# A pair for adaLN units 18 and 19 inside the second value unit of a hybrid encoder layer

## The chip, the core and the metric

The kernel runs on one core of a Trainium2 chip. The time is the device time of one execution in microseconds, as the median of several runs. Times inside an execution come from the hardware profiler's trace; they count from the start of the span.

## What is computed

One encoder layer is computed for 1024 prompt frames and 32 sample frames (1056 columns in all), model width 1024, all in float32. What matters here:

```python
mod = jax.nn.silu(c) @ w_ada + b_ada
sh1, sc1, g1, sh2, sc2, g2 = jnp.split(mod[:, None, :], 6, axis=-1)
h = x * (1 + sc1) + sh1
mq, mk, mv, mo, mi, mf, fq, fk, fv, ff, gu, gv = jnp.split(h @ w_in, split_at, axis=-1)
...
mix = jnp.concatenate([hm, hf, hg], axis=-1) @ w_o
x = _layer_norm(ALPHA * x + (1 + g1) * mix, ln1_g, ln1_b)
h = x * (1 + sc2) + sh2
y = (jax.nn.silu(h @ w_gate) * (h @ w_up)) @ w_down
x = _layer_norm(ALPHA * x + (1 + g2) * y, ln2_g, ln2_b)
```

`mod` (the adaLN modulation) is a product of the two conditioning vectors with a matrix of 1024 x 6144. It is cut into 24 units of 256 columns: units 0 to 7 give sh1 and sc1, units 8 to 15 sh2 and sc2, units 16 to 19 g1, units 20 to 23 g2. g1 is needed only behind the mixers, at the output projection.

## The kernel before

**Engines and queues.** TensorE (PE) does all products, ScalarE (ACT) and VectorE (DVE) empty the PSUM banks and split operands, SyncE (SP) issues nearly all DMAs in one queue, in order. Each product is made of three (hi x hi, lo x hi, hi x lo), L402 to L404 in a value unit and L130 to L132 elsewhere. The program text gives the data flow; a scheduler sets the order of each engine from it, within some fixed dependencies, and so one edit can move instructions that its lines don't name. Each DMA of SP also waits, on its lane (DMAHW0 to DMAHW7), for the DMA issued eight before it.

**An adaLN unit.** `ada_load` (L186) loads the 256 columns as two tiles of 512 KB (L87). `ada_parts` (L193) multiplies them (L202, 8 matmuls in the program, 16 records in the trace), copies the sum from its bank (ACT, L206), transposes it twice on PE (L211), reduces it on DVE (L213), and adds the bias (L219, L223). Up to four units can share one bank, one copy and the two transposes; a group of two is called a pair here.

**The value units.** After the first stage (units 0 to 7 with the first part of the input projection, to about 59 us) come two value units, calls of `tm_unit` (L389) with 264 columns each: the values of the attention heads and the gate columns. A unit has a sample tile (L416) and then tiles 0 to 7, each of 24 products into one of three banks of the pool `pg`. `evac_v` (L423) empties a tile: ACT copies the bank to `tm_traw` (L434, two buffers); SP stores that to the output (`o_v`, 128 KB, L91); DVE splits it into `tm_vhl` (L440, L441, two buffers); SP stores this to `start_dv` (256 KB). So a copy can run only when the store of the tile two before it has landed.

**Where the later adaLN units stand.** Units 16 and 17 are a pair of the function `group` in `run`: its loads go into the pool `pe` (tag `early`, EB = 4 buffers, one unit takes two), and `tie` fixes the matmuls on PE behind tile 0 of the second value unit. `rest` lists the units that follow as single units through `more`: 18 and 19 behind the first step of the gates (`T1[3]` = 2), and 8 to 15 at the eight `a` of ORDER. Their loads go into the pool `pl` (tag `late`, two buffers), so one unit's loads wait until the unit before is done. Behind the value units come the gate columns, the attention heads (`head`, `fox`), the mLSTM chunks, the output projection and the feed-forward part, which takes most of the span.

Of the kernel before, what the change touches and what calls it, by code (L numbers as in the profile page):

```python
# [32 lines left out]
LWE = 1  # L33
NB = (3, 2, 2)
PRE = 5
EB = 4
T1 = (0, 0, 0, 2)
XB, AB = (3, 6)
HPA = 200
MLB = (1, 2, 3, 4, 5)  # L40
# [29 lines left out]
class Kernel:  # L70
# [1428 lines left out]
    def run(self):  # L1499
# [53 lines left out]
        sl = ExitStack()  # L1553
        self.pl = self.pada = self.pool("pl", ctx=sl)
        w1 = d["w_in_v"]
        rest = [18, 19] + list(range(8, 16))

        def more(n):
            for u in rest[:n]:
                self.ada((u,), self.pl, "late", 2, self.pt, "t")  # L1560
            del rest[:n]

        more(T1[0])
        se = ExitStack()
        pe = self.pool("pe", ctx=se, side="right")

        def group(units):
            def go():
                first = len(nc.cur_bb.bb.instructions)
                target = self.lastmm  # L1570
                for _ in self.ada_parts(units, raws, self.pt, "t"):
                    pass
                self.tie(nc.cur_bb.bb.instructions[first:], target, (mybir.EngineType.PE,))
                self.phase = "tm"
            raws = [self.ada_load(u, pe, "early", EB) for u in units]
            return go

        self.tm_unit(w1[0], 264, self.evac_v(0))
        self.tm_unit(w1[1], 264, self.evac_v(1), between={0: group((16, 17))})
        se.close()  # L1580
        s2 = ExitStack()
        self.mx = self.pool("mx0", ctx=s2)
        more(T1[2])
        gates = self.gates()
        next(gates)
        more(T1[3])
        self.foxbufs = (2, 2, 2, 2, 3)
# [278 lines left out]
```

## Time and profile before

| what | value |
|---|---|
| median of 3 runs | 1346.33 us (1344.91 to 1347.18) |
| profiled execution, its own time | 1346.69 us |
| its span from first to last instruction | 1344.9 us |
| PE, ACT, DVE busy | 98%, 49%, 74% of the span |
| granted TensorE clock, mean | 0.998 |
| first value unit's last product on PE | 82.69 us |
| matmuls of units 16 and 17 | 88.01 us |
| matmuls of unit 18 and of unit 19 | 131.45 us and 140.99 us |

A row of the windows view gives a stretch, and the busy time of each engine in it with the number of instructions. A row of a timeline gives start, duration, engine, line, operation, output and inputs, and in brackets how long the engine idled before it and what ended that. `SPq` is the queue on which SP issues DMAs; a row there is the issue, not the transfer. Busy time of matmuls is modelled, so that the steps from start to start say more than durations.

### The profile page before, as it was taken

Reading aid. Unit: us, or ns where it says so; the run is one execution under the profiler, and the core shown is the slowest. Engines: PE = TensorE matmul, PEld = TensorE weight load, DVE = VectorE, ACT = ScalarE, POOL = GpSimd, SP = SyncE. Lnnn points to the kernel's source line nnn. Section 1 sums busy time; section 2 is a strip of 40 time slices with the busy share of each in tenths; the row PEclk is TensorE's granted clock in tenths of the full one; section 3 lists DMA queues with packets and bytes.
Section 4 is the critical chain, followed back from the end, with each engine's and each line's share of the span. In section 5 each row is a group of like instructions: output and inputs, shape, how many; then the busy total and the mean of one; then the engine's idle time right before and its main releaser. Section 6 shows DMA issues by size and latency. Waiting matters only on the chain.

```text
span 1344.9 us, 25607 instructions
## 1 busy us (share of the span) xinstructions
PE 1324.0 (98%) x9684; PEld 1208.3 (90%) x9684; DVE 989.1 (74%) x2091; ACT 655.8 (49%) x1305; POOL 231.9 (17%) x263
## 2 busy tenths in 40 slices
PE   9999999999999999999999999999999999999996
PEld 6798888888999888888888888999999999999995
DVE  5635655678779667686876776678979887988777
ACT  3413445455547545545454454435754453635355
POOL 0102100143246100000000001464610000000341
PEclk9999999999999999999999999999999999999999
DMA  9585465546557754454344332663785858554221
GB/s 362 207 299 154 150 204 186 174 131 207 181 195 257 191 136 130 117 163 126 115 121 116 110 104 82 217 175 112 205 231 154 228 148 225 139 175 131 89 79 67
DMA packets 119450, 221.73 MB, mean 165 GB/s; under 512 B 18580, under 2 KB 62768, under 8 KB 119328
## 3 DMA queue, kind: packets, MB, share of 16 engines
q1 hardware_dynamic: 112096, 207.55, 49.0%
q0 software_dynamic: 6032, 11.94, 5.2%
q8 instruction: 76, 1.25, 0.4%
q10 hardware_dynamic: 1200, 0.62, 0.2%
q14 instruction: 46, 0.38, 0.1%
HBM read 188.13 MB, written 51.85 MB: 178 GB/s over the span
## 4 chain that ended last, share of the span: by engine, by line
PE 68%; DVE 4%; DMA 1%; ACT 1%; issue 1%; DVEq 0%; ACTq 0%
PE up_g L130 6%; PE up_g L132 6%; PE up_g L131 6%; PE dn_g L130 4%; PE dn_g L132 4%; PE dn_g L131 4%; PE sup_u L132 3%; PE sup_u L131 3%; PE sup_u L130 3%; PE wo_g L131 2%; PE wo_g L132 2%; PE wo_g L130 2%; PE sup_g L132 2%; PE sup_g L131 2%; PE sup_g L130 2%; PE fox_t L943 2%
## 5 line engine op out<-in xcount | busy, mean ns | idle before, releaser
L130 PE MATMUL up_g<-tm_ah,up_whi 128*128 128x512 f32 (+1 forms) x384 | 140.0, 365 | 0.0
L131 PE MATMUL up_g<-tm_al,up_whi 128*128 128x512 f32 (+1 forms) x384 | 140.0, 365 | 0.0
L132 PE MATMUL up_g<-tm_ah,up_wlo 128*128 128x512 f32 (+1 forms) x384 | 139.7, 364 | 0.0
L1368 ACT CAST sup_whi<-sup_raw 128x1024 fp32r<-128x1024 f32 x54 | 56.1, 1048 | 89.3 <-PE dn_u L131 43.9
L130 PEld LDWEIGHTS up_g<-tm_ah,up_whi 128*128 128x128 f32 x384 | 72.3, 188 | 11.1 <-DVE tm_al L1246 0.4
L132 PEld LDWEIGHTS up_g<-tm_ah,up_wlo 128*128 128x128 f32 x384 | 72.3, 188 | 11.1
L131 PEld LDWEIGHTS up_g<-tm_al,up_whi 128*128 128x128 f32 x384 | 72.3, 188 | 10.7
L916 ACT ACTIVATE fox_p<-fox_s,fox_fmx 128x384 f32<-128x384 f32 (+2 forms) x96 | 55.2, 579 | 53.0 <-DVE fox_fmx L914 41.2
L1199 DVE SCALAR_TENSOR_TENSOR wo_z<-dn_g,start_mod,wo_z 128x512 f32<-128x512 f32 (+4 forms) x120 | 60.3, 521 | 22.6 <-PE dn_g L132 22.0
L118 DVE TENSOR_TENSOR up_wlo<-up_raw,up_whi 128x1024 fp32r<-128x1024 f32 x50 | 65.2, 1305 | 15.0 <-ACT up_whi L117 13.7
L1369 DVE TENSOR_TENSOR sup_wlo<-sup_raw,sup_whi 128x1024 fp32r<-128x1024 f32 x54 | 68.0, 1263 | 10.7 <-ACT sup_whi L1368 10.7
L117 ACT CAST up_whi<-up_raw 128x1024 fp32r<-128x1024 f32 x50 | 52.4, 1048 | 47.2 <-PE up_g L131 23.9
L130 PE MATMUL dn_g<-up_acth,dn_whi 128*128 128x512 f32 (+2 forms) x200 | 73.5, 368 | 0.8 <-DVE wo_z L1199 0.8
L132 PE MATMUL dn_g<-up_acth,dn_wlo 128*128 128x512 f32 (+2 forms) x200 | 73.3, 366 | 0.0
L131 PE MATMUL dn_g<-up_actl,dn_whi 128*128 128x512 f32 (+2 forms) x200 | 72.8, 365 | 0.0
L948 ACT CAST fox_pth<-fox_t 128x512 fp32r<-128x512 f32 (+1 forms) x80 | 41.6, 542 | 59.2 <-PE fox_t L943 57.5
L117 ACT CAST dn_whi<-dn_raw 128x1024 fp32r<-128x1024 f32 (+1 forms) x44 | 42.7, 971 | 51.7 <-PE up_g L131 16.0
L911 DVE TENSOR_REDUCE fox_fmx<-fox_s 128x1 f32<-128x384 f32 (+2 forms) x96 | 52.8, 553 | 16.3 <-PE fox_s L908 15.0
L949 DVE TENSOR_TENSOR fox_ptl<-fox_t,fox_pth 128x512 fp32r<-128x512 f32 (+1 forms) x80 | 49.9, 631 | 15.9 <-ACT fox_pth L948 15.6
L118 DVE TENSOR_TENSOR dn_wlo<-dn_raw,dn_whi 128x1024 fp32r<-128x1024 f32 (+1 forms) x44 | 49.5, 1125 | 10.4 <-ACT dn_whi L117 9.5
L402 PE MATMUL tm_g<-tm_whi,start_h1h 128*128 128x256 f32 (+1 forms) x192 | 55.3, 288 | 0.7 <-DVE tm_traw L477 0.7
L1320 POOL DMA_DIRECT2D start_dp<-w_gu x19 | 19.8, 1067 | 209.0 <-DMA start_dp<-w_gu 209.0
(684 smaller groups left out, 4799.7 us busy)
## 6 DMA issues: line engine op xcount, KB each, us to landing
up_raw<-w_gu SPq DMA_DIRECT2D x50, 512.0 KB
ada_late<-w_ada SPq DMA_DIRECT2D x28, 512.0 KB
dn_raw<-w_dn SPq DMA_DIRECT2D x28, 512.0 KB
sup_raw<-w_gu SPq DMA_DIRECT2D x20, 512.0 KB
start_dp<-w_gu SPq DMA_DIRECT2D x19, 512.0 KB
start_dp<-w_gu POOLq DMA_DIRECT2D x19, 512.0 KB, 8.0
wo_raw<-w_o SPq DMA_DIRECT2D x18, 512.0 KB
sup_raw<-start_dp SPq DMA_DIRECT2D x18, 512.0 KB
```

The costliest lines, as they stand in the source:

```text
L117: nc.scalar.copy(hi[:, :w], raw[:, :w])
L118: (eng or nc.vector).tensor_tensor(lo[:, :w], raw[:, :w], f(hi[:, :w]), ALU.subtract)
L130: nc.tensor.matmul(ps, hi, xh(k), start=start and k == 0, stop=False)
L131: nc.tensor.matmul(ps, hi, xl(k), start=False, stop=False)
L132: self.lastmm = nc.tensor.matmul(ps, lo, xh(k), start=False, stop=stop and k == n - 1)
L402: nc.tensor.matmul(ps[:, :ncol], xh, hi, start=k == 0, stop=False)
L911: nc.vector.tensor_reduce(mxs[:, x:x + 1], s[:, :w], AX.X, ALU.max, negate=True)
L916: nc.scalar.activation(pr[:, lo:hi], banks[x][:, :hi - lo], AF.Exp, bias=mxs[:, 0:1], accum_out=sums[:, x:x + 1])
L949: nc.vector.tensor_tensor(pl[:, :e], ps[:, :e], f(ph[:, :e]), ALU.subtract)
L1199: self.lastz = self.nc.vector.scalar_tensor_tensor(z[:, m, x:y], ps[:, x - a:y - a], g[i], z[:, m, x:y], ALU.mult, ALU.add)
L1368: nc.scalar.copy(h, x)
L1369: tt(l, x, f(h), ALU.subtract)
```

## The change

Units 18 and 19 leave `rest` and become a second pair of `group`. Its loads are asked for when tile 0 of the second value unit has been written down, behind the first pair; its matmuls are tied behind tile 5 (the sixth). `EB` goes from 4 to 8, so that both pairs have buffers of their own. `T1[3]` goes to 0, and units 8 to 15 keep their places at the `a`.

```diff
-EB = 4
-T1 = (0, 0, 0, 2)
+EB = 8
+T1 = (0, 0, 0, 0)
...
-        rest = [18, 19] + list(range(8, 16))
+        rest = list(range(8, 16))
...
         self.tm_unit(w1[0], 264, self.evac_v(0))
-        self.tm_unit(w1[1], 264, self.evac_v(1), between={0: group((16, 17))})
+        pairs = [group((16, 17))]
+        self.tm_unit(w1[1], 264, self.evac_v(1), between={
+            0: lambda: (pairs[0](), pairs.append(group((18, 19)))), 5: lambda: pairs[1]()})
         se.close()
```

The order of each engine shows what moves. On SP, in the first value unit: the stores of tiles 3 and 4 of the output are `o_v<-tm_traw_854` and `o_v<-tm_traw_887`, the split values' stores are `start_dv`, and `w_ada` is read by the adaLN loads (`tm_early` for the pairs, `ada_late` for single units: unit 18 before, unit 8 after).

```order
 L91 DMA start_dv_59<-tm_vhl_825 128x512
-L87 DMA ada_late_1420<-w_ada 128x1024
-L87 DMA ada_late_1422<-w_ada 128x1024
+L87 DMA tm_early_1117<-w_ada 128x1024
+L87 DMA tm_early_1119<-w_ada 128x1024
 L91 DMA o_v<-tm_traw_854 128x256
+L87 DMA tm_early_1121<-w_ada 128x1024
 L91 DMA start_dv_59<-tm_vhl_858 128x512
+L87 DMA tm_early_1123<-w_ada 128x1024
+L87 DMA ada_late_1819<-w_ada 128x1024
+L87 DMA ada_late_1821<-w_ada 128x1024
 L91 DMA o_v<-tm_traw_887 128x256
```

Unit 18's two loads are replaced by the pair's first two, and four loads of 512 KB come between the stores of tiles 3 and 4. A little ahead of these rows, the first early load of units 16 and 17 now waits for lane DMAHW0 beside its own, which is the lane of the store of `fm_x` from the stage before; before, the store of tile 2 was the first to wait for it.

On ACT, at the end of the first value unit: 920, 953 and 986 are the copies of tiles 5, 6 and 7, `tm_tmsum` that of the second unit's sample tile, 1080 that of its tile 0.

```order
 L434 COPY tm_traw_920<-tm_g_895 128x264 [waits DVE_49,DMAHW6_49,PE_49,Activation_49]
 L117 CAST tm_whi_1010<-tm_raw_1008 128x1056 [waits PE_49]
-L434 COPY tm_traw_953<-tm_g_928 128x264 [waits DMAHW0_49,DVE_49,Activation_49]
-L117 CAST ada_whi_1466<-ada_raw_1464 128x1024 [waits PE_49]
-L434 COPY tm_traw_986<-tm_g_961 128x264 [waits DMAHW2_49,DVE_49,Activation_49]
+L117 CAST gates_whi_1459<-gates_raw_1457 128x1024 [waits PE_49]
 L420 COPY tm_tmsum_1047<-tm_g_1014 32x66 [waits PE_49]
 L420 COPY tm_tmsum_1047<-tm_g_1014 32x66 x3
-L434 COPY tm_traw_1080<-tm_g_1055 128x264 [waits DVE_49,DMAHW4_49,PE_49,Activation_49]
+L434 COPY tm_traw_953<-tm_g_928 128x264 [waits DMAHW4_49,DVE_49,Activation_49]
+L434 COPY tm_traw_986<-tm_g_961 128x264 [waits DMAHW6_49,DVE_49,Activation_49]
```

The copies of tiles 6 and 7 now stand behind those of the sample tile; the lane that the copy of tile 6 waits for is still that of tile 4's store, under another number.

On PE, the new place of units 18 and 19, after the last product of tile 5 (`tm_g_1257`) and ahead of tile 6 of the second value unit:

```order
L404 MATMUL tm_g_1257<-tm_whi_1010,start_h1l_172 128x264
L202 MATMUL ada_t_1290<-tm_early_1119,start_c_62_182 32x256 x4
L202 MATMUL ada_t_1290<-tm_early_1123,start_c_62_182 32x256 x4
L202 MATMUL ada_t_1290<-tm_early_1121,start_c_62_182 32x256 x4
L202 MATMUL ada_t_1290<-tm_early_1117,start_c_62_182 32x256 x4
L402 MATMUL tm_g_1319<-tm_whi_1004,start_h1h_171 128x264
```

And the old place of unit 18 on PE, inside a product of a head's second unit (unit 19 stood the same way some 9 us later, and each had its two transposes):

```order
L130 MATMUL fm_g_1757<-start_h1h_171,gates_whi_1709 128x272
L202 MATMUL ada_t_1424<-ada_late_1422,start_c_62_182 32x256 x4
L202 MATMUL ada_t_1424<-ada_late_1420,start_c_62_182 32x256 x4
L131 MATMUL fm_g_1757<-start_h1l_172,gates_whi_1709 128x272
```

The 16 matmuls now stand together, with one pair of transposes behind them in place of two. From there (104.8 us in the trace of before) to 262 us the pieces of attention, the gates and units 8 and later stand at other places between the same products; ahead of and behind that stretch PE's order is the same in both programs.

## The prediction

> **What bounds the kernel now.** The page comes first: its first part, and the shares of the chain that ended last.
>
> ```profile
> span 1344.9 us, 25607 instructions
> PE 1324.0 (98%) x9684; PEld 1208.3 (90%) x9684; DVE 989.1 (74%) x2091; ACT 655.8 (49%) x1305; POOL 231.9 (17%) x263
> PE 68%; DVE 4%; DMA 1%; ACT 1%; issue 1%; DVEq 0%; ACTq 0%
> ```
>
> TensorE (PE) is busy for 98% of the span, so any time PE stands still is time added at the end, unless a later stall shrinks by as much. The second view is the table of windows, over the stretches in which the order of PE differs (up to 262 us) and the one behind.
>
> ```profile
> 68.00:77.00 9.00, 9.00 (x76) 9.00 (x76) 1.78 (x7) 1.14 (x3) 0.00 (x0) 1.00 1.00 310
> 77.00:82.00 5.00, 5.00 (x43) 5.00 (x43) 0.76 (x3) 0.00 (x0) 0.00 (x0) 1.00 1.03 409
> 82.00:84.00 2.00, 1.34 (x32) 1.12 (x35) 0.38 (x2) 0.80 (x2) 0.00 (x0) 1.00 0.56 206
> 84.00:86.00 2.00, 1.87 (x64) 1.71 (x54) 1.87 (x5) 2.00 (x5) 0.00 (x0) 1.00 0.52 193
> 86.00:105.00 19.00, 19.00 (x174) 17.92 (x173) 7.63 (x34) 3.05 (x11) 0.00 (x0) 1.00 0.77 258
> 105.00:262.00 157.00, 155.90 (x1261) 136.99 (x1261) 93.83 (x265) 77.79 (x183) 13.42 (x22) 1.00 0.55 169
> 262.00:450.00 188.00, 185.30 (x1610) 175.22 (x1609) 150.85 (x347) 99.40 (x216) 82.21 (x84) 1.00 0.62 198
> ```
>
> The columns are window, length, busy us of PE, PEld, DVE, ACT and POOL, granted clock, DMA share, GB/s. From 68 to 82 us the DMA engines are full (share 1.00 and 1.03) while PE is full as well; right behind, at 82 to 86 us, PE loses 0.66 + 0.13 us. The third view, the timelines of SP's queue, ACT and PE, says why.
>
> ```profile
> 68.35 1.29 SPq L87 DMA_DIRECT2D tm_early<-w_ada  x2
> 70.93 0.34 SPq L91 DMA_DIRECT2D o_v<-tm_traw  x1
> 71.32 1.19 SPq L87 DMA_DIRECT2D tm_early<-w_ada  x2
> 72.62 0.51 SPq L91 DMA_DIRECT2D start_dv<-tm_vhl  x1
> 73.19 1.23 SPq L87 DMA_DIRECT2D ada_late<-w_ada  x2
> 74.76 0.37 SPq L91 DMA_DIRECT2D o_v<-tm_traw  x1
> 76.06 0.33 SPq L91 DMA_DIRECT2D start_dv<-tm_vhl  x1
> 76.87 0.34 SPq L91 DMA_DIRECT2D o_v<-tm_traw  x1
> ```
>
> ```profile
> 76.46 0.38 ACT L434 COPY tm_traw<-tm_g 128x264 f32<-128x264 f32 x1 [4.68 <-DMA o_v<-tm_traw]
> 83.20 0.38 ACT L434 COPY tm_traw<-tm_g 128x264 f32<-128x264 f32 x1 [6.37 <-DMA o_v<-tm_traw]
> 83.48 1.08 ACT L117 CAST tm_whi<-tm_raw 128x1056 fp32r<-128x1056 f32 x1
> 84.46 0.38 ACT L434 COPY tm_traw<-tm_g 128x264 f32<-128x264 f32 x1
> ```
>
> ```profile
> 82.69 0.29 PE L404 MATMUL tm_g<-tm_whi,start_h1l 128*128 128x264 f32 x1
> 83.64 1.13 PE L416 MATMUL tm_g<-tm_raw,start_hs 128*32 128x66 f32 x64 [0.66 <-ACT tm_traw L434]
> 84.89 0.39 PE L402 MATMUL tm_g<-tm_whi,start_ah 128*128 128x264 f32 x1
> ```
>
> I count the tiles of a value unit from 0. The copies at 76.46, 83.20 and 84.46 empty the banks of tiles 4, 5 and 6 of the first value unit. The one at 83.20 had waited 6.37 us for the store of tile 3, because traw has two buffers. That store was issued at 74.76 and holds 131 KB, which is 0.3 us at 409 GB/s; it took 8.4 us since it stood behind six loads of 512 KB. PE's sample tile at 83.64 needs the bank that this copy frees, since the products have three banks in turn; tile 0 of the second unit, at 84.89, needs the bank of tile 6, copied at 84.46, which in turn needs the store of tile 4 (issued 76.87). So here the program is at the edge already: **PE waits for ACT, ACT for a small store, the store for big loads.**
>
> **The change part by part.** *Removed PE work.* Two single units become a pair.
>
> ```profile
> 131.23 0.29 PE L130 MATMUL fm_g<-start_h1h,gates_whi 128*128 128x272 f32 x1
> 131.45 1.07 PE L202 MATMUL ada_t<-ada_late,start_c 128*32 128x256 f32 x16
> 132.68 0.28 PE L132 MATMUL fm_g<-start_h1h,gates_wlo 128*128 128x272 f32 x1
> 132.81 0.29 PE L130 MATMUL fm_g<-start_h1h,gates_whi 128*128 128x272 f32 x1
> ...
> 87.80 0.28 PE L404 MATMUL tm_g<-tm_whi,start_al 128*128 128x264 f32 x1
> 88.01 1.93 PE L202 MATMUL ada_t<-tm_early,start_c 128*32 128x256 f32 x32
> 90.11 0.29 PE L403 MATMUL tm_g<-tm_wlo,start_ah 128*128 128x264 f32 x1
> ...
> 135.33 0.29 PE L132 MATMUL fm_g<-start_h1h,gates_wlo 128*128 128x272 f32 x1
> 135.46 0.38 PE L211 MATMUL ada_t<-start_ident,ada_adas 128*128 128x128 f32 x2
> 135.80 0.28 PE L131 MATMUL fm_g<-start_h1l,gates_whi 128*128 128x272 f32 x1
> ```
>
> A single unit costs PE 132.68 - 131.23 = 1.45 us less two ordinary steps of 0.125, so 1.20. A pair costs 90.11 - 87.80 = 2.31 less two steps of 0.12, so 2.07. Two transposes cost 135.80 - 135.33 = 0.47 less two steps, so 0.22. The saving is 2 x 1.20 - 2.07 + 0.22 = **0.55 us**. One copy on ACT and one reduction with its share of small operations on DVE go too; ACT (49%) and DVE (74%) have room there, so I cost them at nothing.
>
> *Moved loads.* This is the term that decides. In the new order of SP four loads of 512 KB (the second unit of the pair, and unit 8, whose buffers are now free from the start) stand between the stores of tiles 3 and 4 of the first unit; before, none did. They are 4 x 524,288 B = 2.10 MB. At 409 GB/s, the rate of the same stretch, they take 5.13 us; at the 310 GB/s of 68 to 77 us, 6.77 us. I take 409, since they would run right behind that stretch, in a queue as full. Issue is no limit: the DMA that the tile 4 store's lane waits for is the first load of the pair, five big transfers earlier.
>
> Before, the store of tile 4 landed after 83.20 and before 84.46; behind the store of tile 3 it had one store of 262 KB and its own 131 KB to move, 0.96 us at 409 GB/s, so I take 84.16 (an estimate from these rows). After, it lands at 84.16 + 5.13 = 89.29. From the start of a copy to PE is 83.64 - 83.20 = 0.44 us, so tile 0 starts at 89.73 and not at 84.89: **+4.84 us**. The ends are +3.9 (landing just after 83.20) and +6.5 (310 GB/s). Behind the waiting copy on ACT stand the copy of tile 7 and then the pair's own copy; on PE stands everything.
>
> *The later start of the train.* With the new pool the first early load also waits for the store of fm_x (lane DMAHW0). Before, that lane's next user, the store at 70.93, had it by then, and the load had gone at 68.35. So the start slips by 0 to 2.6 us. The queue was full but slow then (310 against 409 GB/s), so most of a slip is caught up: I take +0.4 us.
>
> *No second stall.* The copy of tile 7 waits for tile 5's store, which follows tile 4's after 0.4 MB (about 1 us); the bank that it frees is needed 2.9 + 2.07 us after 89.73. The first copy of the second unit waits for tile 6's store, which stands behind three weight loads (1.57 MB, 3.9 us) and lands near 96; its bank is needed by tile 3, near 100. The loads of units 18 and 19 land near 88 and are used near 109. So I cost these at nothing; without the margin every 512 KB ahead of a store would cost 1.28 us.
>
> *The order from 105 to 262 us* is reshuffled: attention and adaLN pieces stand at other places between the same products. Before, PE idles there for 157.00 - 155.90 = 1.10 us, so at most that can go; the stretch behind it idles 2.70 of 188.00, and a new order could cost 1.6 more. Bounds -1.1 to +1.6; I take 0. Behind 262 us the order of PE is the same to the end, and it passes a shift on: 86 to 105 is full, and the idle of 105 to 450 (3.8 us) waits on engines that PE feeds.
>
> **Sum:** -0.55 + 4.84 + 0.4 + 0 = +4.69 us on the profiled execution's 1346.69 (span 1344.9 and 1.8 around it), 1351.4 us. The median of the runs shown is 0.36 lower than that execution, so I forecast 1351.0.
>
> [...]
>
> **The rivals.** *The stall also slows the clock (0.22).* From the end of the sample tile to 89.73 PE would stand still for about 4.9 us, a length that the trace shows only once.
>
> ```profile
> 1332.00:1334.00 2.00, 1.21 (x6) 0.67 (x4) 0.68 (x2) 0.82 (x3) 0.00 (x0) 1.00 0.01 4
> 1336.00:1338.00 2.00, 0.00 (x0) 0.00 (x0) 1.93 (x6) 1.31 (x3) 0.00 (x0) 1.00 0.00 0
> 1338.00:1341.00 3.00, 0.00 (x0) 0.00 (x0) 2.90 (x8) 2.35 (x5) 0.00 (x0) 0.54 0.56 186
> ```
>
> At the end PE's last matmul ends near 1333.2; the granted clock stays at 1.00 past 1338 and has a mean of 0.54 to 1341, so it fell to half near 1338.2, after 5.0 us. My gap is just under that. If it falls, the next tile (24 products, from 84.89 to a step behind 87.80, 3.0 us) runs at half speed and costs 3.0 more: 1354.0 us. [...]
>
> *The stores do not wait for the loads (0.12).* If packets of the small store get through between the loads, tile 4's store lands by 84.46 as before and only the saving is left: 1345.8 us, not slower. It decides at one point: does the store land within 0.4 us of the old time? For it speaks only that no view lists the packets one by one, so the order inside the queue is inferred. Against it: the store at 74.76 took 8.4 us behind six loads, and the one at 70.93, for which the copy at 76.46 waited, 5.5 us behind two.
>
> *The stall is partly given back (0.16).* The landing at its early end (-0.9) and the idle time of 105 to 262 us gone (-1.1): 1349.0 us, on the border of 0.2%. That the pair might not form is no rival: the order of PE shows its 32 matmuls behind tile 5.
>
> **How the numbers follow.** The forecast has 0.50, and the time is its 1351.0. Less than 0.2% (2.7 us) is about what a measurement of this kernel can tell from no change. The forecast and the clock rival are slower (0.72), and half of the give-back (0.08), less 0.02 for luck in the reshuffled order: 0.78. Same: most of the free-store case and the other half, 0.19. Faster needs 2.7 us, with no stall, where the saving and the bound of the reshuffled order give 1.65: 0.03, for bounds that are wrong. The range 1347.3 to 1354.5 takes in give-back, clock rival and the bounds that do not all fall together; it leaves out the free-store case and the far upper end.
>
> **What would show it.** Right: in ACT's timeline a wait of tm_traw for the o_v store that ends near 89, and PE's tile 0 of the second unit starting near 89.7 with 4 to 6 us idle before it, the rest shifted by a constant. The SP queue then shows o_v behind four loads, and the pair of units 18 and 19 one insertion of 2.07 us near 109. Wrong: a tile 0 start before 86; a granted clock under 1.00 in 88 to 95 (the clock rival); or idle time in 105 to 262 that moves by more than 1.6 us.

## The result, and the profile after

The changed kernel takes 1349.55 us in the median of 13 runs (1345.07 to 1351.83), the kernel before 1346.12 us (13 runs, 1344.05 to 1348.96). The ratio is 1.0024, with a 95% interval of 1.0015 to 1.0032: slower by 3.2 us (2.0 to 4.3). The sign held, and the time lies in the range, 1.5 us under the forecast of 1351.0 us. The sum behind it did not hold term by term: two of its terms were wrong by about the same amount in opposite directions.

The page of the changed kernel shows nothing of this; PE is at 98% as before.

```profile
span 1347.8 us, 25594 instructions
PE 1324.7 (98%) x9682; PEld 1210.0 (90%) x9682; DVE 988.9 (73%) x2090; ACT 656.0 (49%) x1304; POOL 233.5 (17%) x263
```

The windows around the stall do (columns as in the prediction: window, length, PE, PEld, DVE, ACT, POOL, granted clock, DMA share, GB/s):

```profile
82.00:84.00 2.00, 1.18 (x10) 0.96 (x8) 0.15 (x1) 0.00 (x0) 0.00 (x0) 1.00 1.04 405
84.00:86.00 2.00, 1.13 (x64) 0.96 (x64) 0.45 (x2) 1.66 (x3) 0.00 (x0) 1.00 1.03 418
86.00:88.00 2.00, 0.56 (x2) 0.56 (x3) 2.00 (x3) 1.35 (x5) 0.00 (x0) 0.57 1.02 410
88.00:90.00 2.00, 2.00 (x11) 2.00 (x10) 0.92 (x4) 0.00 (x0) 0.00 (x0) 0.50 1.08 412
90.00:92.00 2.00, 2.00 (x11) 2.00 (x10) 0.91 (x4) 0.76 (x2) 0.00 (x0) 0.50 0.99 358
92.00:94.00 2.00, 2.00 (x25) 1.39 (x28) 0.11 (x1) 0.00 (x0) 0.00 (x0) 0.72 0.99 330
94.00:96.00 2.00, 2.00 (x29) 1.40 (x22) 0.00 (x0) 0.37 (x1) 0.00 (x0) 1.00 0.83 309
```

Two things are to be seen. PE loses 0.82 + 0.87 + 1.44 us in the first three windows, where the kernel before lost 0.79 in all. And the granted clock is at half from 86 to 93 us: in 88 to 90 us PE is "busy" all the time with 11 matmuls, where the kernel before has 17 to 19 in each 2 us from 90 to 96 us at a clock of 1.00. The DMA queue is full from 82 to 90 us (share 1.02 to 1.08, 405 to 418 GB/s); that it stands behind both is what the experiments test.

ACT's timeline, at the end of the first value unit:

```profile
84.34 0.38 ACT L434 COPY tm_traw<-tm_g 128x264 f32<-128x264 f32 x1 [7.43 <-DMA o_v<-tm_traw]
84.61 1.08 ACT L117 CAST tm_whi<-tm_raw 128x1056 fp32r<-128x1056 f32 x1
85.59 1.05 ACT L117 CAST gates_whi<-gates_raw 128x1024 fp32r<-128x1024 f32 x1
86.53 0.85 ACT L420 COPY tm_tmsum<-tm_g 32x66 f32<-32x66 f32 x4
90.58 0.38 ACT L434 COPY tm_traw<-tm_g 128x264 f32<-128x264 f32 x1 [3.19 <-DMA o_v<-tm_traw]
```

The first and the last row are the copies of tiles 5 and 6. They started at 83.20 and 84.46 before; now the second waits for the store of tile 4 until 90.58. That is the long wait for an `o_v` store that the prediction asked for. But PE did not wait for that copy:

```profile
82.89 0.29 PE L404 MATMUL tm_g<-tm_whi,start_h1l 128*128 128x264 f32 x1
84.77 1.13 PE L416 MATMUL tm_g<-tm_raw,start_hs 128*32 128x66 f32 x64 [1.59 <-ACT tm_traw L434]
87.44 0.59 PE L402 MATMUL tm_g<-tm_whi,start_ah 128*128 128x264 f32 x1 [1.54 <-ACT tm_tmsum L420]
92.67 0.42 PE L404 MATMUL tm_g<-tm_whi,start_al 128*128 128x264 f32 x1
93.02 1.95 PE L202 MATMUL ada_t<-tm_early,start_c 128*32 128x256 f32 x32
95.13 0.29 PE L403 MATMUL tm_g<-tm_wlo,start_ah 128*128 128x264 f32 x1
```

Tile 0 of the second unit starts at 87.44, released by the copies of the sample tile (L420), which end there; tile 6's copy comes 3.1 us later. Tile 0 then runs from 87.44 to 92.89, with 0.22 us between steps in place of 0.12 (11 matmuls in 88 to 90 us).

To follow the shift, the same instruction is read in both traces. The last product of the first unit stands at 82.69 before and 82.89 now (0.20 apart since the first stage of the run). The L403 behind the first pair stands at 90.11 before and 95.13 now, 5.02 later. So the stall and the slow tile cost 4.82 us together: 2.55 - 0.20 = 2.35 to the start of tile 0 (84.89 to 87.44), and 2.47 from there to the pair and tile 1. Of the 2.35 us, 0.93 came ahead of the sample tile (1.59 us idle in place of 0.66). The rest came behind it: its matmuls ended at 85.90, and its copies started only at 86.53, behind the two casts on ACT.

### The profile page after: what moved, and what is told of

It reads as the page before. It is cut to its first block, busy times and chain, and to the rows that moved or that the text cites. A ratio compares the mean times of both kernels' runs of the same rounds, so it can differ in the third digit from the quotient of the medians.

```text
span 1347.8 us, 25594 instructions
## 1 busy us (share of the span) xinstructions
PE 1324.7 (98%) x9682; PEld 1210.0 (90%) x9682; DVE 988.9 (73%) x2090; ACT 656.0 (49%) x1304; POOL 233.5 (17%) x263
## 4 chain that ended last, share of the span: by engine, by line
PE 69%; DVE 4%; DMA 2%; issue 0%; ACT 0%; SPq 0%; DVEq 0%; ACTq 0%
PE up_g L130 6%; PE up_g L132 6%; PE up_g L131 6%; PE dn_g L130 4%; PE dn_g L132 4%; PE dn_g L131 4%; PE sup_u L132 3%; PE sup_u L131 3%; PE sup_u L130 3%; PE wo_g L130 2%; PE wo_g L132 2%; PE wo_g L131 2%; PE sup_g L131 2%; PE sup_g L132 2%; PE sup_g L130 2%; PE fox_t L943 2%
## 5 line engine op out<-in xcount | busy, mean ns | idle before, releaser
L402 PE MATMUL tm_g<-tm_whi,start_ah 128*128 128x256 f32 (+1 forms) x192 | 56.3, 294 | 2.1 <-ACT tm_tmsum L420 1.5
L404 PE MATMUL tm_g<-tm_whi,start_al 128*128 128x256 f32 (+1 forms) x192 | 55.6, 290 | 0.0
```

Source lines behind the costliest of these rows:

```text
L402: nc.tensor.matmul(ps[:, :ncol], xh, hi, start=k == 0, stop=False)
L404: self.lastmm = nc.tensor.matmul(ps[:, :ncol], xl, hi, start=False, stop=k == 7)
```

## Where the shift goes later

Further on two rows of PE are compared: the first sample tile behind 320 us, and the last matmul of the run. The kernel before:

```profile
322.72 1.10 PE L416 MATMUL tm_g<-tm_raw,start_hs 128*32 128x64 f32 x64 [1.04 <-DVE tm_traw L477]
1332.59 0.62 PE L1083 MATMUL lnb_t<-dn_tmp,start_onesm 128*128 128x272 f32 x2
```

The changed kernel:

```profile
327.11 1.10 PE L416 MATMUL tm_g<-tm_raw,start_hs 128*32 128x64 f32 x64 [1.08 <-DVE tm_traw L477]
1335.51 0.62 PE L1083 MATMUL lnb_t<-dn_tmp,start_onesm 128*128 128x272 f32 x2
```

The lag is 5.02 at 90 us, 4.39 at 322 and 2.92 at the end. The matched rows between show where it changes: +2.28 at the new pair (its matmuls and transposes), -1.42 at each of the two single units that are gone, which is -0.56, the saved work; +4.48 at 262 us; and -1.9 between 960 and 1011 us, where the prediction had nothing. There the profiled execution of the kernel before waited, as the first of these rows shows; the second is the changed kernel.

```profile
1000.00:1020.00 20.00, 18.88 (x146) 18.34 (x145) 14.89 (x34) 7.40 (x12) 3.09 (x3) 1.00 0.83 225
```

```profile
1000.00:1020.00 20.00, 20.00 (x159) 19.90 (x158) 16.48 (x36) 7.94 (x14) 2.06 (x2) 1.00 0.92 252
```

PE idled 1.12 us there, behind DVE and ACT, and ACT had waited 5.07 us for a load of the down projection's weights:

```profile
1003.84 0.84 ACT L117 CAST dn_whi<-dn_raw 128x768 fp32r<-128x768 f32 x1 [5.07 <-DMA dn_raw<-w_dn]
```

Is that wait slack, which swallows part of any delay, or the luck of one execution? The experiments ask this too.

## The theories and the experiments

Theory A: the four loads ahead of tile 4's store make the stall, and the stall, not the new order of PE, is what costs. Within A the halved clock is a part of its own, which can be taken away while the stall stays. Rival B: the cost lies in the new order of PE from 105 to 262 us. Rival D: the eight buffers alone do it, by the later start of the load train. Runs of the kernel before stand beside each kernel, on the same chip: their median is 1346.12 us for the first four kernels below, 1344.83 for the half dummies, the assumed order and the version that beats both, and 1345.33 for the delay, the second executions and the last one. Ratios are to those runs.

### Four buffers for the early loads: the loads move, PE's order stays

```diff
-EB = 8
+EB = 4
```

> The changed kernel with four early buffers in place of eight. PE's order is that of the changed kernel, row for row; only DMAs move: the second pair's four loads now wait for the first pair's matmuls, so that no big load stands between the stores of tiles 3 and 4 of the first value unit. Theory A (the four big loads ahead of tile 4's store make the stall at 82 to 95 us, and the halved clock there comes from that stall): tile 0 of the second unit starts near 84.9, tile 1 near 89.9, the granted clock stays at 1.00, and the time is that of the kernel before less the saved work, 1345.6 us, some 4 us under the changed kernel. Rival B (the cost lies in the new order of PE between 105 and 262 us and in the pair's place): PE's order is the same as in the changed kernel, so the time stays near 1349.5. Rival C (the second pair's loads only move the stall): a new wait of PE of 2 us or more for data of the second pair near 109 us or for a store near 100 us, and 1347.5 to 1349.

1346.14 us, ratio 0.9997 (0.9989 to 1.0006). PE:

```profile
84.40 1.13 PE L416 MATMUL tm_g<-tm_raw,start_hs 128*32 128x66 f32 x64 [0.68 <-ACT tm_traw L434]
88.78 1.93 PE L202 MATMUL ada_t<-tm_early,start_c 128*32 128x256 f32 x32
```

The run is 0.75 us late since its first stage; beyond that the rows from 82 to 100 us are those of the kernel before, with the old wait of 0.68 us, tile 0 in 3.1 us and the clock at 1.00. The order of PE is the changed kernel's, and it costs nothing: the lag goes from 0.76 at 90 us to 0.28 at 262 us, which is the saved work. B falls, and so does C, since no new wait shows at 100 or 109 us. What the edit takes away is the eight buffers and, with them, the place of the four loads; the next two kernels part these.

### Eight buffers alone

```diff
-EB = 4
+EB = 8
```

(in the kernel before)

> The kernel before with eight early buffers and nothing else changed; the first early load then also waits for the store of fm_x. Theory A: the load train starts up to 2.6 us later, and the four loads of the second pair are not there; tile 4's store lands 0 to 0.5 us later, the time is 1346.1 to 1346.6, no change that can be measured. Rival D (the later start alone makes the stall): tile 0 of the second unit starts 1.5 us or more later than 84.9, and the time is 1348 or above.

1347.66 us, ratio 1.0011 (1.0002 to 1.0019). PE:

```profile
84.33 1.13 PE L416 MATMUL tm_g<-tm_raw,start_hs 128*32 128x66 f32 x64 [1.06 <-ACT tm_traw L434]
312.99 1.08 PE L762 MATMUL mlstm_s<-mlstm_mv,mlstm_mw 128*128 128x65 f32 x8 [1.89 <-DMA mlstm_mv<-start_dmv]
```

Around the stall A is right: the wait for the bank grows from 0.66 to 1.06 us, by the 0.4 that the prediction gave the later start, and D's 1.5 us do not show. The median is nevertheless 1.5 us up (0.3 to 2.6), more than A expected. In this execution 1.89 us went at 313 us to a load, in no row that the edit touches, and 1.8 us more to small waits from 320 to 450 us (PE busy 126.08 us there, 127.85 in the kernel before); the kernel with only the first five dummies, below, had the same wait at 313 us. Whether eight buffers bring this about is open. They need not cost anything: the next two kernels have eight buffers as well, and their times are, within their intervals, those of the kernel before.

### Four output buffers, with the loads where they are

```diff
-            raw = self.t(self.sm, [P, 264], F32, "traw", 2)
+            raw = self.t(self.pe, [P, 264], F32, "vraw", 4)
...
-        pe = self.pool("pe", ctx=se, side="right")
+        pe = self.pe = self.pool("pe", ctx=se, side="right")
```

> The changed kernel whose value tiles have four output buffers (in the pool of the early loads) in place of two, so that a copy waits for the store four tiles back. The four loads stay where they are. Theory A: no copy on ACT waits for a store near 82 to 91 us, tile 0 starts at 84.9 or up to 0.7 us earlier (the 0.66 us that the kernel before waits there goes too), clock 1.00, time 1344.9 to 1345.6. Rival B: the time stays near 1349.5, since PE's order behind 105 us is that of the changed kernel but for a few rows. Rival E (the loads hurt by another way, for instance the second half of the split values' stores or late weights): the wait moves to another DMA and the time is 1347 or more.

1345.97 us, ratio 1.0005 (0.9994 to 1.0015). The stall is gone although the four loads stand where they stood: from 70 to 100 us PE's lag against the kernel before falls by 0.53 us, most of the old wait of 0.66, and where the changed kernel stood still PE is full:

```profile
86.00:88.00 2.00, 2.00 (x59) 1.91 (x48) 1.12 (x3) 1.72 (x6) 0.00 (x0) 1.00 1.03 410
```

But the new buffers lie in space that the stage before still held. Their first copy waited for a store of that stage, and PE stood still for 1.8 us behind it:

```profile
70.27 0.94 ACT L434 COPY tm_vraw<-tm_g 128x264 f32<-128x264 f32 x3 [8.84 <-DMA o_vs<-start_vs]
```

So A holds for the stall: the same loads at the same rate (410 GB/s) cost nothing where no copy waits for a store behind them. The time over the expectation is no more than this side effect of the experiment. Of B this kernel says little, as its order of PE from 105 to 262 us differs from the changed kernel's at many places; the four-buffer kernel, which has that order row for row, decides there.

### Dummy matmuls in the stall

```diff
+            warm = getattr(self, "warm", (0, 0))
+            self.dummies(warm[0])
             self.sample_tile(self.raws, ncol, evac)
+            self.dummies(warm[1])
...
+    def dummies(self, n):
+        if n:
+            first = len(self.nc.cur_bb.bb.instructions)
+            ps = self.t(self.pss, [P, 512], F32, "s")
+            for _ in range(n):
+                self.nc.tensor.matmul(ps[:, :P], self.onesm, self.onesm, start=True, stop=True)
+            self.tie(self.nc.cur_bb.bb.instructions[first:], self.lastmm, (mybir.EngineType.PE,))
...
+        self.warm = (5, 5)
         self.tm_unit(w1[1], 264, self.evac_v(1), between={
             0: lambda: (pairs[0](), pairs.append(group((18, 19)))), 5: lambda: pairs[1]()})
+        self.warm = (0, 0)
```

> The changed kernel with ten dummy matmuls (128x128 into a spare bank, of no use to the output), five ahead of the sample tile of the second unit and five behind it, where PE stands still anyhow. Theory A with the clock as a part of its own: PE is kept busy through the stall, the granted clock stays at 1.00 over 86 to 94 us, tile 0 takes 3.0 us in place of 5.5, and tile 1 starts near 92.4 in place of 94.9; the time is 2.5 us less than the changed kernel, 1347.1. If the slow tile has another cause (late operands, DMA traffic on the memory of the operands): tile 0 still takes 5.5 us and the time stays at 1349.5 or grows by up to 0.5.

1346.01 us, ratio 1.0001 (0.9992 to 1.0009). PE, and one window:

```profile
82.44 1.28 PE L417 MATMUL tm_s<-start_onesm 128*128 128x128 f32 x10
83.78 1.13 PE L427 MATMUL tm_g<-tm_raw,start_hs 128*32 128x66 f32 x64
84.84 1.38 PE L417 MATMUL tm_s<-start_onesm 128*128 128x128 f32 x10
86.45 0.39 PE L405 MATMUL tm_g<-tm_whi,start_ah 128*128 128x264 f32 x1 [0.24 <-ACT tm_tmsum L431]
89.58 1.93 PE L202 MATMUL ada_t<-tm_early,start_c 128*32 128x256 f32 x32
```

```profile
88.00:90.00 2.00, 2.00 (x22) 1.72 (x24) 0.20 (x2) 0.38 (x1) 0.00 (x0) 1.00 0.99 361
```

Useless work in the gap makes the kernel faster: its interval lies wholly below the changed kernel's. The waits for the banks are still there (the copies of the sample tile release tile 0 at 86.45), but the clock stays at 1.00 and tile 0 takes 86.45 to 89.58, 3.1 us in place of 5.6. The time fell by 3.5 us, some more than the 2.5 expected; the intervals allow that.

### Half of the dummies

The same with the five dummies ahead of the sample tile alone (`warm` at 5, 0), or behind it alone (0, 5), one execution each.

> The changed kernel with the five dummy matmuls ahead of the sample tile alone; the idle 1.5 us behind the sample tile stays. If the clock is halved by the length of one idle stretch or by the last one: it falls to 0.50 near 87 to 90 as in the changed kernel, and tile 0 takes 5 us or more. If it is the idle time summed over some us that halves it (1.6 + 1.5 us idle in 4.6 us of the changed kernel): one gap of 1.5 us is not enough, the clock stays at 1.00 and tile 0 takes 3.0 us, 1347.1 us by the profile.

> The changed kernel with the five dummy matmuls behind the sample tile alone; the idle 1.6 us ahead of it stays. By the sum of idle time: clock 1.00 through 84 to 94 us, tile 0 takes 3.0 us. By one stretch: a gap of 1.6 us ahead of the sample tile halves the clock near 85 to 88 us, and the dummies and tile 0 run at 0.22 us a step in place of 0.12.

Both kept the clock at 1.00 from 82 to 100 us. With the first five alone:

```profile
86.20 0.39 PE L405 MATMUL tm_g<-tm_whi,start_ah 128*128 128x264 f32 x1 [1.33 <-ACT tm_tmsum L431]
88.00:90.00 2.00, 2.00 (x25) 1.60 (x27) 0.18 (x2) 0.38 (x1) 0.00 (x0) 1.00 1.07 420
```

With the second five alone PE stood 0.67 us ahead of the sample tile and 0.23 behind it:

```profile
88.00:90.00 2.00, 2.00 (x20) 1.79 (x22) 0.27 (x3) 0.00 (x0) 0.00 (x0) 1.00 1.06 409
```

So one gap of 1.33 us did not halve the clock in that execution. That both arms kept it is no proof that only the sum of the idle time counts: the changed kernel itself kept its clock in another execution, shown further on. The second arm says less than planned, since its gap was 0.67 and not 1.6 us. The times of the two arms were 1348.04 and 1346.12 us; the first lost 1.9 us at 313 us, as the eight buffers alone did.

### The order that the prediction assumed

The copies of the sample tile are held behind those of tiles 6 and 7 on ACT, as in the kernel before. The rows of PE and SP around them stay as they were.

```diff
-            nc.scalar.copy(raw, ps[:, :264])
+            self.lastcopy = nc.scalar.copy(raw, ps[:, :264])
...
+        first = len(nc.cur_bb.bb.instructions)
         for q in range(4):
             nc.scalar.copy(r[:, n * q:n * q + n], ps[32 * q:32 * q + 32, :n])
+        if ncol == 264 and hasattr(self, "lastcopy"):
+            self.tie(nc.cur_bb.bb.instructions[first:], self.lastcopy, (mybir.EngineType.Activation,))
```

> The changed kernel with the copies of the sample tile on ACT held behind the copies of tiles 6 and 7, as they stood in the kernel before; PE's and SP's rows are those of the changed kernel. This is the order that the prediction assumed: tile 0 of the second unit then waits for the bank of tile 6, and so for the store of tile 4. If the prediction's step was wrong only in this place: tile 0 starts near 91.0 (0.44 us behind the copy of tile 6, which started at 90.58 in the changed kernel) in place of 87.44, 3.6 us more idle, the clock falls to half in the gap, and tile 1 starts near 98; the time is 1352 to 1353.5. If tile 0 gets its bank elsewhere: it starts within 1 us of 87.44 and the time stays at 1349.5.

1353.04 us (1352.32 to 1354.04), ratio 1.0062 (1.0049 to 1.0075). PE and ACT:

```profile
83.74 1.13 PE L416 MATMUL tm_g<-tm_raw,start_hs 128*32 128x66 f32 x64 [0.94 <-ACT tm_traw L437]
90.73 0.59 PE L402 MATMUL tm_g<-tm_whi,start_ah 128*128 128x264 f32 x1 [5.87 <-ACT tm_traw L437]
96.07 1.93 PE L202 MATMUL ada_t<-tm_early,start_c 128*32 128x256 f32 x32
```

```profile
90.30 0.38 ACT L437 COPY tm_traw<-tm_g 128x264 f32<-128x264 f32 x1 [4.70 <-DMA o_v<-tm_traw]
91.25 0.38 ACT L437 COPY tm_traw<-tm_g 128x264 f32<-128x264 f32 x1 [0.57 <-DVE tm_vhl L443]
91.53 0.86 ACT L421 COPY tm_tmsum<-tm_g 32x66 f32<-32x66 f32 x4
```

Now tile 0 takes tile 6's bank and starts 0.43 us behind its copy. The chain of the prediction, run as it was assumed, gives 90.73, where it forecast 89.73 and up to 0.4 more. Behind the gap of 5.87 us the clock is at half as well (0.50 from 90 to 94 us), and the kernel is 8.2 us slower than the one before.

### How much of a delay reaches the end

18 dummy matmuls in the kernel before, behind tile 2 of the second value unit; the rows around them stay as they were.

```diff
-        self.tm_unit(w1[1], 264, self.evac_v(1), between={0: group((16, 17))})
+        self.tm_unit(w1[1], 264, self.evac_v(1), between={0: group((16, 17)),
+                                                             2: lambda: self.dummies(18)})
...
```

> The kernel before with 18 dummy matmuls (128x128 into a spare bank, some 0.25 us each, 4.6 us) behind tile 2 of the second value unit, and every other row of every engine where it was. It asks how much of a delay of PE near 98 us reaches the end. If a delay is passed on whole, as the prediction assumed: PE 4.6 us late at 262, 450, 960 and 1330 us, and 1350.7 us in the median. If part is given back: less than 4.6 at 1330 us, by the wait of 1.1 us for the down projection's weights at 1004 to 1011 us (with its tail 1.7 us) and by the waits of 262 to 450 us, and 1348.5 to 1349.5.

> The kernel before once more, for a second profile. If the wait near 1004 to 1011 us, which the changed kernel's profile lacks, belongs to the kernel before: it is there again, 1.1 us of idle PE in 1006 to 1012 us. If it comes and goes from execution to execution: it is gone or another size.

> The changed kernel once more, for a second profile. If what was seen there belongs to the kernel: tile 0 of the second unit behind the copies of the sample tile (1.5 us idle), the granted clock 0.50 from 86 to 93 us, tile 1 near 94.9, and no wait at 1004 to 1011 us.

The delayed kernel took 1348.47 us, ratio 1.0025 (1.0016 to 1.0034), 3.1 us by the medians and 3.4 by the ratio (2.2 to 4.6). Its rows:

```profile
87.39 1.93 PE L202 MATMUL ada_t<-tm_early,start_c 128*32 128x256 f32 x32
95.43 4.18 PE L413 MATMUL tm_s<-start_onesm 128*128 128x128 f32 x36
1333.93 0.62 PE L1090 MATMUL lnb_t<-dn_tmp,start_onesm 128*128 128x272 f32 x2
```

A second profiled execution of the kernel before:

```profile
88.40 1.93 PE L202 MATMUL ada_t<-tm_early,start_c 128*32 128x256 f32 x32
1000.00:1020.00 20.00, 20.00 (x160) 19.90 (x158) 17.74 (x39) 7.66 (x13) 2.06 (x2) 1.00 0.87 211
1330.59 0.62 PE L1083 MATMUL lnb_t<-dn_tmp,start_onesm 128*128 128x272 f32 x2
```

The delay measured 4.04 us by the matched rows on both sides of it, and not 4.6. Against that execution the delayed kernel is 1.01 us early ahead of the dummies, 3.02 late behind them and 3.34 late at the last matmul: in this pair of profiles nothing of it is swallowed on the way. The medians leave this open. They put 3.1 us at the end, at the edge of what was expected for a delay given back in part, where 4.04 passed on whole would give 1349.4 us; the interval of 2.2 to 4.6 us takes in both.

The wait at 1004 us is not in the second execution of the kernel before, nor in that of the delayed kernel. PE idled 1.40 us there in the four-buffer kernel, 0.60 with the first five dummies alone and 0.59 in the faster version of the next section with the pair; in that version without the pair and with all ten dummies, not at all. Some of these executions ran late and some early, on both sides. So the wait comes and goes from execution to execution, and lateness alone does not decide it. By this the 1.9 us "given back" above belong to the execution that was profiled before and not to the change. Against the second execution of the kernel before, the changed kernel's profile is 1335.51 - 1330.59 = 4.92 us late at the end.

A second profiled execution of the changed kernel took 1345.79 us:

```profile
84.16 1.13 PE L416 MATMUL tm_g<-tm_raw,start_hs 128*32 128x66 f32 x64 [0.98 <-ACT tm_traw L434]
86.83 0.39 PE L402 MATMUL tm_g<-tm_whi,start_ah 128*128 128x264 f32 x1 [1.54 <-ACT tm_tmsum L420]
89.95 1.93 PE L202 MATMUL ada_t<-tm_early,start_c 128*32 128x256 f32 x32
```

The same waits for the same copies, the first one shorter (0.98 us for 1.59), but the clock stayed at 1.00 and tile 0 took 3.1 us. This execution's last matmul stands 1.08 us behind that of the kernel before's second execution, the one with the halved clock 4.92. The measured 3.2 us lie between. The mean clock of single runs points the same way: it was 0.996 or less in 12 of 13 runs of the changed kernel, and in 15 of 71 of the kernel before. As 6.8 us at half clock lower a mean by 0.0025, this is a hint and no count.

### A version that beats both

Four early buffers, and the odd tiles of the value units in two output buffers of their own, so that four serve in turn and the first copy waits for no space; and the same buffers in the kernel before, without the pair.

```diff
-EB = 8
+EB = 4
...
-            raw = self.t(self.sm, [P, 264], F32, "traw", 2)
+            raw = (self.t(self.pe, [P, 264], F32, "vraw", 2) if tt % 2 else
+                   self.t(self.sm, [P, 264], F32, "traw", 2))
...
-        pe = self.pool("pe", ctx=se, side="right")
+        pe = self.pe = self.pool("pe", ctx=se, side="right")
```

> A version meant to beat both: the changed kernel with four early buffers, and the odd tiles of the value units in two output buffers of their own in the pool of the early loads, so that four buffers serve the copies in turn. Theory A: the saved work (0.5 us) and the wait of 0.66 us at 83 us are gone: 1344.9 us, ratio 0.999. Against: the early loads start behind fewer stores, and the first odd copy waits for space that the stage before holds (the four buffers in that pool cost 1.8 us near 70 us): then 1346 to 1348.

> The kernel before with the four output buffers of the version that beat it (odd tiles of the value units in two buffers of their own), and no second pair: it parts that version's gain (1343.65 against 1344.83). If the gain is the wait at 82 to 84 us: 0.7 us less than the kernel before. If the pair's saving of 0.5 us and its order of PE from 105 to 262 us make the most of it: within 0.3 us of the kernel before plus or minus the 0.7, and behind 262 us the lead is 1 us smaller than in that version.

With the pair 1343.65 us, ratio 0.9986 (0.9977 to 0.9995); without it 1343.63, ratio 0.9990 (0.9981 to 0.9999). In both the sample tile follows the last product without a wait; with the pair it reads:

```profile
83.24 1.13 PE L416 MATMUL tm_g<-tm_raw,start_hs 128*32 128x66 f32 x64
```

Both are faster than the kernel before, and the four buffers alone give nearly as much. Their 1.3 us by the ratio (0.1 to 2.6) are more than the wait of 0.66 us that they take away, but the interval takes that in. The 0.5 us of the pair are too small to be told from the two intervals.

## Why the prediction was right, and which of its steps failed

- **Stores behind loads: right.** The four loads moved the store of tile 4: the copy that waits for it started at 90.58, for 89.29 + 0.4 forecast. The two copies stand 6.24 us apart. Before, by the prediction's estimate, 0.96 us lay between the two landings, so the loads added 5.3, for 5.13. The rate was 405 to 418 GB/s, for 409 taken.
- **The bank: the step that failed.** "tile 0 of the second unit, at 84.89, needs the bank of tile 6, copied at 84.46, which in turn needs the store of tile 4": this sentence of the prediction describes the kernel before. In the changed order the sample tile's copies stand ahead of tile 6's on ACT, and tile 0 takes the bank that comes free first by that order. The rows of ACT shown with the change had the new order of the copies; the prediction read them only for the lane. It was 2.35 us to the start of tile 0, and not 4.84 + 0.4. With the old order of those copies tile 0 started at 90.73.
- **The clock: costed at nothing, and a rival at 0.22.** It fell, though no gap came near the 4.9 us that the rival took for its condition: 1.59 us idle, the sample tile, 1.54 us idle. The price was 2.47 us, for 3.0. The dummies and the second execution show that it is a cost of its own. The prediction itself had named a clock under 1.00 in 88 to 95 us as a sign of being wrong, and a start of tile 0 near 89.7 as one of being right; the profile shows the first and, with 87.44, not the second.
- **The sum.** 2.35 + 2.47 = 4.82, where 4.84 + 0.4 stood for the first alone: 2.89 us too much for the wait, 2.47 too little for the clock. The time came out near by this accident, and so by luck; the second execution, with the same waits at full clock, came out 1.08 us late. Had tile 0 waited as assumed, 1351.0 would have been too low by the clock's share, as the kernel with the assumed order showed.
- **The later start of the load train: right in size, as far as the scatter lets one say.** +0.4 forecast. The wait ahead of the sample tile was 0.66 us in one execution of the kernel before and 0.44 in the other; eight buffers alone had 1.06, the changed kernel 1.59 and 0.98.
- **Issue is no limit: right for the time, not in the letter.** SP issued tile 4's store only at 82.69, as loads ahead of it waited for the DMA eight before them (the one issued at 79.47 for 2.5 us); the transfers ran on without a gap all the same (405 to 418 GB/s from 82 to 90 us).
- **The saved work: right.** -0.55 forecast; the matched rows give +2.28 - 2 x 1.42 = -0.56, and the four-buffer kernel -0.48 up to 262 us.
- **The reshuffled order at 0: right.** 5.02 - 0.56 = 4.46, and the lag at 262 us was 4.48.
- **A shift is passed on: right in the profiles**, by the delay of 4.04 us; the medians, with 3.1, leave some give-back open. Waits for loads at 313 and at 1004 us, up to 1.9 us each, come and go between executions. A comparison of two profiles holds them as if they were the change's.
- **The free stores (0.12) fell**, as the store of tile 4 landed some 6 us later than before. The give-back (0.16) has the time nearest to the measured one, 1349.0 us, but neither of its conditions held: the landing came late and not early, and the idle time of 105 to 262 us was 0.97 us, for 1.10 before.

## What to carry to other kernels

Where an edit reorders an engine's queue, the question to ask of each wait is not which buffer it used before but which one the new order frees first; the order of the engine that empties the buffers answers it. A short stall on PE can cost more than its length, here 2.47 us more by the halved clock in one of two executions, and ten useless matmuls in the gap were worth 3.5 us. And one pair of profiles is good for places, but a second execution of each kernel is needed before a difference far from the edit is called an effect.

## What the runs showed of the hardware

- The granted clock fell to half without a long gap: in the changed kernel from about 86.3 us (0.57 in the window of 86 to 88) to 93.1 (0.72 in 92 to 94), 6.8 us. The two ends are worked out from the means, with 1.00 and 0.50 as the levels. Ahead of the fall lay 1.59 us idle, 64 small matmuls in 1.1 us, and 0.4 us of the next idle stretch. With 5.87 us idle in one piece it fell too. The windows of the kernel with that gap, the one with the assumed order:

```profile
88.00:90.00 2.00, 0.00 (x0) 0.00 (x0) 0.00 (x0) 0.00 (x0) 0.00 (x0) 0.72 1.08 417
94.00:96.00 2.00, 2.00 (x11) 1.93 (x10) 0.41 (x2) 0.00 (x0) 0.00 (x0) 0.57 0.57 212
```

  This is from 88.9 to 95.7, again 6.8 us, and 4.0 us after the last matmul. The changed kernel kept its clock at 1.00 from 82 to 96 us in a second execution, which idled 2.52 us there in place of 3.13; whether that is why, no run shows. How much work in a gap keeps the clock up is open; no run here varied it finely.
- A gap of 1.33 us next to dense work left the clock at 1.00 in the one execution that had it, and so did 0.98 + 1.54 us in the second execution of the changed kernel.
- A store of 131 KB took 7.9 us from its issue at 82.69 to the copy that waited for it at 90.58, with big loads ahead of it in the queue.
